# Encoder step: three places for x in the front, the memory's norms spread out, a gate's weights asked for one chunk earlier

## The chip, the cores and the metric

The kernel runs on one core of one Trainium2 chip. The engines named here are TensorE (PE in the rows; PEld is its weight load), VectorE (DVE), ScalarE (ACT), GpSimd (POOL) and SyncE (SP), which only issues DMAs here. The metric is the device time of one launch in microseconds, the median of the runs of a kernel.

## The reference, cut to what matters

The layer takes 1024 prompt tokens and 8 x 16 = 128 sample tokens, width 1024, in fp32. What the change touches is the normed input, its projections, the memory's keys and values, the forget gates and the output gates.

```python
xn = rmsnorm(xp, g_mix[l])
z = xn @ w_in                       # split into qa, ka, va, qb, kb, vb, fl, qm, gates
logf = jax.nn.log_sigmoid(fl.astype(jnp.float32) + b_f.astype(jnp.float32))
...
mk, mv = jnp.split(rmsnorm(mem, g_mem) @ w_mkv, 2, axis=-1)
return rmsnorm(mk.reshape(b, n, H_M, DH_M), g_km), mv.reshape(b, n, H_M, DH_M)
...
o_a = band_attn_prompt(qa, ka, va, rel_bias[l])
o_b = forget_attn_prompt(qb, kb, vb, lf)
o_m = mem_attn(qm, mk, mv)
xp = xp + gated_merge(o_a, o_b, o_m, gates, w_pa[l], w_pb[l], w_pm[l], w_o[l])
xp = xp + sq_relu_mlp(xp, g_ffn[l], w_up[l], w_down[l])
```

The sample tokens go the same way with cached keys and values.

## The kernel before

**Precision.** Most projections are made of three products of fp32r halves: an operand is split into `hi` (rounded) and `lo` (the rest), and TensorE adds hi·whi, hi·wlo and lo·whi in PSUM. ACT makes a `hi`, scaled by the gain where there is one (`gcol`), and DVE the `lo`; `hilo_scaled` does both for one k of 128 rows.

**The front.** x comes in transposed, in five pieces of 256 tokens (`x_load(t)`; piece 4 holds the 128 sample tokens, "the sample tile", token tile 8). Each lands in a place of the arena `FE` (`x_place`) and is split by `x_split(t)` into `xp`. A place is free again when the sums of the piece for the products (`sums`) are made on DVE. The rows of x are loaded a second time, not transposed, by `x_rows`: ACT squares them, POOL takes the root, and `rs` scales what leaves PSUM. Meanwhile TensorE multiplies the token tiles in the order 0, 1, 8, 2 to 7 with the weights of v_a and the forget gates (`wa` and `sb` in the rows; their raw form lies in the arena `RW`); `v_a` evacuates each tile's banks (`z`) on ACT to `zn`, which waits for `rs`, and DVE takes the forget columns to `lf`. All these loads are issued by SP in the order in which the code asks for them, so one that waits for its place holds back all behind it.

**Products and memory.** Four projections follow as `products(...)`, which form sums of weights and of tokens to save matmuls, and then the memory's keys (`mem_products(104, ...)`, with `mem_k`) and values (`mem_products(112, ...)`, with `mem_v`). The work behind a result (`norm`: square on ACT, sum `hss` on DVE, root `hr` on POOL, product `zn` on DVE, transposes `to_T` on TensorE) is put off by `in_(n, ...)` until `flush()` has been called n times, so that TensorE has matmuls between. The places of four raw weights, `kept`, hold their weights longer than others for the products' sums, and x again later: `odd_x(t)` splits the first half of token tile 2t+1 once more from there, during the memory's keys.

**The planned phase.** From the first gate on, each engine's order comes of a planner in the kernel that runs generators against estimated costs (`plan.use`, `plan.op`) and times (`plan.t`). TensorE's filler there are the gates: 24 blocks f of output columns by three chunks c of 384 tokens, 24 matmuls each. `get(f)` asks for the weights of gate f in two halves: ACT issues the DMA into the one staging buffer `wst`, ACT makes `whi` of it and DVE or POOL `wlo`; buffers stand for two gates. Beside them run the band attention ("attention a"), the forget attention, the sample attentions, then the merge with memory attention, and last the output projection and the MLP (L1863), which the change leaves alone. `forget_gates` turns `lf` into log sigmoids, about twenty short operations on DVE, and transposes the result.

PE and DVE follow the order of the code in the front, too, from `in_order.extend((pe, vec))` on. ACT and POOL are ordered by a scheduler there.

## Time and profile before

| | us |
|---|---|
| median of 3 runs | 2014.13 |
| lowest and highest run | 2010.42, 2015.04 |
| profiled execution, whole | 2010.68 |
| its span in the trace | 2008.9 |
| around the span (difference) | 1.78 |
| PE busy in the span | 1954.7 |
| DVE / ACT / POOL busy | 1221.4 / 946.0 / 521.1 |

The profiled execution is near the lowest of the runs. Mean granted TensorE clock over it: 0.989. A row's time is its start from the beginning of the span; "idle before" is the idle time of that engine just ahead of the row, and behind the arrow stands what ended it. The granted clock (PEclk) is a share of full speed, 2.4 GHz.

### The profile page before, as it was taken

How to read it: one execution, taken by the hardware profiler on the slowest of the kernel's cores; microseconds unless marked ns; L12 is line 12 of the kernel's file. 1: busy time of each engine (PE TensorE's matmuls, PEld its weight loads, DVE VectorE, ACT ScalarE, POOL GpSimd, SP SyncE). 2: the span in 40 equal slices, each digit the busy share in tenths (PEclk: the TensorE clock that was granted, in tenths of full speed). 3: DMA queues.
4: the chain of work that ended last, by engine and by line, in shares of the span. 5: the costliest groups of instructions: out<-in, count | busy, mean ns of one | idle time of the engine just before them, and what ended most of it. 6: DMA issues, size and time to landing. Idle time of an engine off the chain costs nothing.

```text
span 2008.9 us, 33955 instructions
## 1 busy us (share of the span) xinstructions
PE 1954.7 (97%) x12338; PEld 1712.1 (85%) x12338; DVE 1221.4 (61%) x2313; ACT 946.0 (47%) x1831; POOL 521.1 (26%) x590
## 2 busy tenths in 40 slices
PE   8999999899999999998899999999999999999999
PEld 8887888788887988887898987889999998888887
DVE  7766657665632555522575843876666665785775
ACT  6645556455643556533452313644444454453332
POOL 3343433332311244311122200244443431000000
PEclk9999999999999999999898999999999999999999
DMA  8555455643259433278658453144343459563463
GB/s 264 162 156 180 117 168 150 203 152 102 80 164 316 154 104 98 68 245 278 196 179 282 153 162 113 46 157 157 127 141 129 143 169 330 183 197 106 128 197 126
DMA packets 223909, 330.54 MB, mean 165 GB/s; under 512 B 32357, under 2 KB 109302, under 8 KB 223742
## 3 DMA queue, kind: packets, MB, share of 16 engines
q1 hardware_dynamic: 166600, 270.44, 42.3%
q10 hardware_dynamic: 57142, 57.93, 8.7%
q8 instruction: 97, 1.59, 0.3%
q14 instruction: 70, 0.57, 0.1%
HBM read 243.11 MB, written 85.18 MB: 163 GB/s over the span
## 4 chain that ended last, share of the span: by engine, by line
PE 77%; DMA 10%; DVE 6%; ACT 2%; issue 2%; POOL 2%; SPq 1%; ACTq 0%; POOLq 0%; DVEq 0%
PE b L1863 36%; PE z L215 28%; PE tp L222 5%; PE tp L215 4%; PE s L215 4%; DMA wst<-in_w_g 2%; DMA th<-tg 1%; POOL fa L203 1%; DVE r L203 1%; DVE fa L203 1%; DVE lo L203 1%; DMA kd<-in_cak 1%; DMA fa<-in_w_up 1%; SPq L203 1%; DMA tg<-tg 1%
## 5 line engine op out<-in xcount | busy, mean ns | idle before, releaser
L1863 PE MATMUL b<-r 128*128 128x512 f32 (+2 forms) x2200 | 457.6, 357 | 4.2 <-ACT r L203 2.1
L1863 PEld LDWEIGHTS b<-r 128*128 128x128 f32 x2200 | 379.6, 190 | 62.6 <-DVE r L203 3.6
L203 ACT ACTIVATE r<-fa 128x512 fp32r<-128x512 f32 (+4 forms) x264 | 212.8, 816 | 327.2 <-PE b L1863 280.9
L203 DVE TENSOR_TENSOR r<-fa,r 128x512 fp32r<-128x512 f32 (+4 forms) x264 | 273.5, 1047 | 136.1 <-ACT r L203 131.9
L215 PE MATMUL z<-hi,whi 128*128 128x384 f32 x960 | 320.2, 365 | 15.0 <-ACT hi L203 8.0
L1863 PE MATMUL b<-r,r 128*128 128x320 f32 (+1 forms) x1928 | 288.3, 299 | 5.8 <-DVE r L203 5.7
L1863 PEld LDWEIGHTS b<-r,r 128*128 128x128 f32 x1928 | 271.2, 190 | 7.7 <-DVE r L203 7.7
L215 PE MATMUL z<-hi,wlo 128*128 128x384 f32 x768 | 262.0, 341 | 0.2
L203 POOL TENSOR_TENSOR fa<-fa 128x512 f32<-128x512 f32 x114 | 165.2, 1455 | 238.4 <-ACT fa L203 125.5
L215 PEld LDWEIGHTS z<-hi,whi 128*128 128x128 f32 x960 | 180.5, 193 | 39.4 <-issue 15.1
L215 PE MATMUL z<-wa,hi 128*128 128x512 f32 (+1 forms) x732 | 203.5, 365 | 6.4 <-ACT hi L203 4.7
L215 PE MATMUL z<-lo,whi 128*128 128x384 f32 x576 | 195.1, 339 | 0.0
L215 PEld LDWEIGHTS z<-wa,hi 128*128 128x128 f32 x732 | 128.7, 192 | 27.2 <-ACT hi L203 5.1
L215 PEld LDWEIGHTS z<-hi,wlo 128*128 128x128 f32 x768 | 146.7, 191 | 1.3 <-DVE wlo L203 1.3
L203 ACT ACTIVATE s<-s,nm 128x256 f32<-128x256 f32 (+8 forms) x180 | 121.2, 679 | 39.1 <-DVE nm L203 38.9
L203 POOL TENSOR_SCALAR s<-s,ri 128x256 f32<-128x256 f32 (+8 forms) x108 | 76.0, 709 | 232.1 <-DVE ri L203 208.7
L215 PE MATMUL z<-wa,lo 128*128 128x512 f32 (+1 forms) x366 | 130.5, 359 | 0.0
L203 DVE CUSTOM_DVE_ANT_0 s<-s,bias 128x384 f32<-128x384 f32 (+4 forms) x144 | 70.4, 526 | 84.3 <-PE s L215 81.3
L215 PEld LDWEIGHTS z<-lo,whi 128*128 128x128 f32 x576 | 109.8, 191 | 0.0
L222 PE MATMUL tp<-ident,s 128*128 128x128 f32 (+1 forms) x680 | 107.3, 277 | 1.7 <-ACT pt L203 1.2
L203 ACT ACTIVATE pt<-tp 128x256 f32<-128x256 f32 (+3 forms) x153 | 66.4, 454 | 80.6 <-PE tp L222 76.8
L203 DVE TENSOR_TENSOR fa<-b,fa 128x256 f32<-128x256 f32 (+1 forms) x160 | 70.5, 448 | 54.0 <-PE b L1863 39.1
(223 smaller groups left out, 3136.4 us busy)
## 6 DMA issues: line engine op xcount, KB each, us to landing
td<-fa SPq DMA_DIRECT2D x112, 256.0 KB
rw<-in_w_in SPq DMA_DIRECT2D x104, 256.0 KB
fa<-td SPq DMA_DIRECT2D x80, 256.0 KB
fa<-in_w_down SPq DMA_DIRECT2D x76, 256.0 KB
fa<-in_w_up SPq DMA_DIRECT2D x32, 512.0 KB
tg<-tg ACTq DMA_DIRECT2D x72, 192.0 KB
th<-tg SPq DMA_DIRECT2D x72, 192.0 KB
wst<-in_w_g ACTq DMA_DIRECT2D x48, 256.0 KB
```

The lines of the kernel that those rows point to most:

```text
L203: ins = f(*a, **k)
L215: ins = nc.tensor.matmul(out, lhsT, rhs, **k)
L222: ins = nc.tensor.transpose(*a)
L1863: pin(nc.tensor.matmul(ps, lh, rh, **k))
```

## The change

It has four parts.

1. **Front.** x has three places in `FE` in place of two (`t % 3`). The rows of x go to `RW` at first, where the raw weights have been used up, and to free parts of `FE` later (`row[1]`). The sample tile is loaded and split ahead of the first rows; piece 2 is asked for after token tile 0, piece 3 after token tile 1, behind the loads of the `kept` weights and two rows.
2. **Memory.** `norm` of a memory tile squares into one of two `zt` buffers in place of the one `sq`; the delays become 3, and the memory's values flush after every k. `odd_x` runs at k = 2 to 5 and uses `hilo_scaled`.
3. **Forget gates.** They begin 30 us later in the planner's time, and their cost is put at 6.0 in place of 3.0.
4. **Gates.** The weights of gate f+1 are asked for at chunk 0 of gate f; before it was chunk 1, but for gate 22's. Gate 23's are asked for at (22, 0) in both.

```diff
--- before.py
+++ after.py
@@ -375,7 +375,7 @@
     def x_place(t):
 
         return FE[:, 4096:5120].rearrange("p (k t) -> p k t", k=8) if t == 4 else \
-            FE[:, t % 2 * 2048:t % 2 * 2048 + 2048].rearrange("p (k t) -> p k t", k=8)
+            FE[:, t % 3 * 2048:t % 3 * 2048 + 2048].rearrange("p (k t) -> p k t", k=8)
 
     def x_load(t, ks=slice(0, 8)):
         sp.dma_start(x_place(t)[:, ks, :], xT[:, ks, t * 256:min(t * 256 + 256, NT)])
@@ -391,7 +391,7 @@
             x += n
 
     def row_sums(src, s, r, e):
-        xt = FE[:, 4096 + e * D:4096 + e * D + D]
+        xt = row[1][:, e * D:e * D + D]
         sp.dma_start(xt, src)
         act.activation(xt, xt, AF.Square, accum_out=s)
         rstd(s, r, D)
@@ -401,7 +401,7 @@
             row_sums(i["x"][t * P:(t + 1) * P, :], ss[:, t:t + 1], rs[:, t:t + 1], row[0])
             row[0] = 1 - row[0]
 
-    row = [1]
+    row = [1, RW]
 
 
 
@@ -590,11 +590,11 @@
             if len(ks) > 1:
                 flush()
 
-    def norm(z, sc, dh, then, gain=None, fresh=False):
+    def norm(z, sc, dh, then, gain=None, fresh=False, lag=2):
 
         nh = HB // dh
         v3 = lambda t: t.rearrange("p (h d) -> p h d", h=nh)
-        sq = tl(pj, (P, HB), tag="sq", bufs=1)
+        sq = tl(pj, (P, 4, P), tag="zt").rearrange("p k t -> p (k t)") if fresh else tl(pj, (P, HB), tag="sq", bufs=1)
         act.activation(sq, z, AF.Square, scale=sc)
         r = tl(pj, (P, 8), tag="hr", bufs=4)
 
@@ -603,7 +603,7 @@
             vec.tensor_reduce(q[:, :nh], v3(sq), AX.X, ALU.add)
             rstd(q[:, :nh], r[:, :nh], dh)
             gps.tensor_scalar(r[:, :nh], r[:, :nh], sc, 1.0, ALU.mult, ALU.mult)
-            in_(2, scale)
+            in_(lag, scale)
 
         def scale():
             zn = tl(pj, (P, HB), tag="zn") if fresh else z
@@ -644,8 +644,8 @@
     def mem_k(t, z):
         def then(zn):
             sp.dma_start(o["mk"][t * P:(t + 1) * P, :], zn)
-            in_(2, lambda: to_T(zn, mkT, t))
-        norm(z, rm[:, t:t + 1], 128, then, g_of["km"], True)
+            in_(3, lambda: to_T(zn, mkT, t))
+        norm(z, rm[:, t:t + 1], 128, then, g_of["km"], True, 3)
 
     mem_v = v_out(o["mv"], rm, True)
 
@@ -721,12 +721,12 @@
         x_load(0, slice(k, k + 1))
         produce((slots + more)[k], vec if k < 2 else gps)
         x_split(0, (k,))
-    x_rows(0)
-    sp.dma_start(bf, i["b_f"].to_broadcast((P, 8)))
     x_load(4)
     x_split(4)
+    x_rows(0)
     x_load(1, slice(0, 4))
     x_load(1, slice(4, 8))
+    sp.dma_start(bf, i["b_f"].to_broadcast((P, 8)))
     x_rows(1)
     x_split(1)
     x_rows(TT - 1)
@@ -735,8 +735,6 @@
         makers_of(pair, PAIRS[n + 1] if n < 2 else None)
     queue.extend(i["w_mkv"][k * P:(k + 1) * P, x:x + HB] for x in (0, HB) for k in range(KD))
     makers.extend([take] * 16)
-    for k in range(4):
-        sp.dma_start(kept[k], rows_(Q_A)(k))
     sp.dma_start(ident, i["ident"])
     for x, y, n in ((0, 128, 128), (128, 384, 128)):
         sp.dma_start(gains[:, x:x + n], i["gains"][0:1, y:y + n].to_broadcast((P, n)))
@@ -762,21 +760,30 @@
             z.append(ps)
         v_a(t, z[0], z[1][:, 0:252])
         vec.scalar_tensor_tensor(lf[:, t, :], z[1][:, 252:260], rs[:, t:t + 1], bf, ALU.mult, ALU.add)
+        if t == 0:
+            x_load(2, slice(0, 4))
+            x_load(2, slice(4, 8))
+            x_rows(2, 3)
+            x_split(2)
         if t in (1, 3, 5):
             for step in sums(t // 2):
                 step()
-            if t < 5:
-                x_load(t // 2 + 2, slice(0, 4))
-                x_load(t // 2 + 2, slice(4, 8))
-                x_split(t // 2 + 2)
-                x_rows(t + 1, t + 2)
             if t == 1:
+                for k in range(4):
+                    sp.dma_start(kept[k], rows_(Q_A)(k))
+                row[1] = RW[:, 6 * UW:]
+                x_rows(4, 5)
+                x_load(3, slice(0, 4))
+                x_load(3, slice(4, 8))
                 ask()
+                x_split(3)
             if t == 3:
+                row[1] = FE[:, 2048:4096]
                 x_rows(6, 7)
+    row[1] = FE[:, 4096:6144]
     for t in range(2):
         row_sums(i["mem"][t * P:(t + 1) * P, :], ss[:, TT + t:TT + t + 1], rm[:, t:t + 1], t)
-    T2, u2, u3 = ([FE[:, (4 * j + t) * HB:(4 * j + t + 1) * HB] for t in range(4)] for j in range(3))
+    u2, u3, T2 = ([FE[:, (4 * j + t) * HB:(4 * j + t + 1) * HB] for t in range(4)] for j in range(3))
     sp.dma_start(tri, i["tri"])
 
     def rs_T():
@@ -801,8 +808,9 @@
     def odd_x(t):
 
         x = kept[t].rearrange("p (k t) -> p k t", k=4)
-        vec.tensor_tensor(x, x, gcol[:, 0, 0:4, None].to_broadcast((P, 4, P)), ALU.mult)
-        into_odd(t, x)
+        h, l = odd(t)
+        for k in range(4):
+            hilo_scaled(x[:, k, :], h[:, k, :], l[k], gcol[:, 0, k:k + 1])
 
     def at_last(t):
 
@@ -831,10 +839,12 @@
                 pe.matmul(ps[t], h, wl, start=False, stop=False)
                 pe.matmul(ps[t], l, wh, start=False, stop=k == KD - 1)
             release(u0 + k)
-            if k % 2:
+            if u0 != 104:
                 flush()
-                if u0 == 104:
-                    odd_x(k // 2)
+            elif k % 2:
+                flush()
+            if u0 == 104 and 1 < k < 6:
+                odd_x(k - 2)
         for t in range(2):
             out(t, ps[t])
 
@@ -848,6 +858,7 @@
 
     def forget_gates(pool):
 
+        yield plan.t + 30.0
         z = lf.rearrange("p t h -> p (t h)")
         n = TT * 8
         w = {k: tl(pool, (P, n), tag="f" + k) for k in "aesuvr"}
@@ -874,7 +885,7 @@
         vec.tensor_tensor(v, v, s, ALU.mult)
         vec.tensor_scalar(z, z, 0.0, None, ALU.min)
         vec.tensor_tensor(z, z, v, ALU.subtract)
-        yield plan.use("vec", 3.0)
+        yield plan.use("vec", 6.0)
         act.dma_start(o["lf"].rearrange("(t p) h -> p t h", p=P), lf)
         bk = plan.take("tp")
         t = tl(psum["tp"], (P, 4, P), tag="tp")
@@ -962,7 +973,7 @@
                 if k == 0:
                     b = plan.take("z")
                     ps = tl(psum["z"], (P, 512), tag="z")
-                    if (f, c) == (22, 0) or c == 1 and f < 22:
+                    if c == 0 and f < 23:
                         plan.spawn(get(f + 1), own=False)
                     if (f, c) == (23, 0):
                         late["start"]()
```

SP's queue in the front, from the last of v_a's weights on (`fe<-in_xT` are pieces of x, `in_x` rows of x, and the `rw<-in_w_in` of 128x512 the kept weights). Before:

```order
L203 DMA fe_268<-in_x 128x1024
L203 DMA bf_210<-in_b_f 128x8
L203 DMA fe_268<-in_xT 128x8x128
L203 DMA fe_268<-in_xT 128x4x256 x2
L203 DMA fe_268<-in_x 128x1024 x2
L203 DMA rw_252<-in_w_in 128x512 x4
...
L203 DMA gq_244<-in_gains 128x1
L203 DMA fe_268<-in_x 128x1024 x2
L203 DMA fe_268<-in_xT 128x4x256 x2
L203 DMA rw_252<-in_w_in 128x512 x6
```

And now:

```order
L203 DMA fe_268<-in_xT 128x8x128
L203 DMA rw_252<-in_x 128x1024
L203 DMA fe_268<-in_xT 128x4x256 x2
L203 DMA bf_210<-in_b_f 128x8
L203 DMA rw_252<-in_x 128x1024 x2
...
L203 DMA gq_244<-in_gains 128x1
L203 DMA fe_268<-in_xT 128x4x256 x2
L203 DMA rw_252<-in_x 128x1024 x3
L203 DMA rw_252<-in_w_in 128x512
L203 DMA rw_252<-in_x 128x1024
L203 DMA rw_252<-in_w_in 128x512 x3
L203 DMA fe_268<-in_xT 128x4x256 x2
```

The sample tile's load stands ahead of the first row, piece 2 directly behind the constants, and the kept weights behind piece 2; piece 3 comes behind them.

ACT in the front, from the last split of v_a's weights (`sb`) on (`hi_163` and `hi_164` are the sample tile, `hi_143`, `hi_144`, `hi_153` and `hi_154` piece 1, `ss` the sums of squares). Before:

```order
L203 ACTIVATE sb_264<-rw_252 128x520
L203 ACTIVATE fe_268,ss_243<-fe_268 128x1024
L203 ACTIVATE sa_260<-fe_268 128x512
L203 ACTIVATE zn_476<-z_426,rs_241 128x260
L203 ACTIVATE zn_476<-z_451,rs_241 128x252
L203 ACTIVATE hi_163_231<-fe_268,gcol_201 128x128 x4
L203 ACTIVATE hi_164_232<-fe_268,gcol_201 128x128 x4
L203 ACTIVATE hi_143_211<-fe_268,gcol_201 128x128 x4
```

And now:

```order
L203 ACTIVATE sb_264<-rw_252 128x520
L203 ACTIVATE hi_163_231<-fe_268,gcol_201 128x128 x4
L203 ACTIVATE hi_164_232<-fe_268,gcol_201 128x128 x4
L203 ACTIVATE rw_252,ss_243<-rw_252 128x1024
L203 ACTIVATE hi_143_211<-fe_268,gcol_201 128x128 x4
...
L203 ACTIVATE rw_252,ss_243<-rw_252 128x1024
L203 ACTIVATE hi_154_222<-fe_268,gcol_201 128x128 x4
L203 ACTIVATE rw_252,ss_243<-rw_252 128x1024
L203 ACTIVATE zn_472<-z_422,rs_241 128x260
L203 ACTIVATE zn_472<-z_447,rs_241 128x252
```

The eight `hi` of the sample tile moved ahead of the first square; the evacuation of token tile 0 (`zn`) moved behind 24 `hi` and three squares.

TensorE at the end of the memory's values and the begin of gate 0 (`wa,sa` are the values' matmuls, one row of three for each of two tiles and each k; `tp<-ident,zn` transposes the memory's normed keys). Before:

```order
L215 MATMUL z_3696<-wa_256,sa_260 128x512 x3
L215 MATMUL z_3697<-wa_256,sa_260 128x512 x3
L215 MATMUL z_3696<-wa_256,sa_260 128x512 x3
L215 MATMUL z_3697<-wa_256,sa_260 128x512 x3
L222 MATMUL tp_3785<-ident_203,zn_3747 128x128 x4
L222 MATMUL tp_3793<-ident_203,zn_3751 128x128 x4
L215 MATMUL z_3839<-hi_143_211,whi_3775 128x384
```

And now:

```order
L215 MATMUL z_3704<-wa_256,sa_260 128x512 x3
L215 MATMUL z_3705<-wa_256,sa_260 128x512 x3
L222 MATMUL tp_3769<-ident_203,zn_3743 128x128 x4
L222 MATMUL tp_3777<-ident_203,zn_3747 128x128 x4
L215 MATMUL z_3704<-wa_256,sa_260 128x512 x3
L215 MATMUL z_3705<-wa_256,sa_260 128x512 x3
L215 MATMUL z_3839<-hi_143_211,whi_3799 128x384
```

The transposes moved ahead of the last k. The forget gates' transpose moved the other way: some 256 matmuls later, from the second chunk of gate 0 into attention a.

## Rows read from the trace of the kernel before

**Rows 1.** The page, part 1: busy time, share of the span and instructions of each engine.

```profile
PE 1954.7 (97%) x12338; PEld 1712.1 (85%) x12338; DVE 1221.4 (61%) x2313; ACT 946.0 (47%) x1831; POOL 521.1 (26%) x590
```

**Rows 2.** Timeline of PE in the front: start us, us, instruction, idle before.

```profile
22.43 0.75 PE L215 MATMUL z<-wa,hi 128*128 128x260 f32 x4 [2.55 <-ACT hi L203]
...
43.77 1.10 PE L215 MATMUL z<-wa,hi 128*128 128x260 f32 x5 [2.13 <-ACT hi L203]
```

**Rows 3.** Windows, PE alone: length, PE busy (matmuls started), PEclk, DMA share, GB/s.

```profile
23.70:27.20 3.50, 3.50 (x19) 0.51 0.39 128
27.20:30.70 3.50, 3.50 (x31) 1.00 0.99 323
44.20:47.70 3.50, 3.50 (x19) 0.51 1.06 398
```

**Rows 4.** Timeline of ACT in the front.

```profile
21.98 6.24 ACT L203 ACTIVATE hi<-fe,gcol 128x128 fp32r<-128x128 f32 x21
...
43.21 1.70 ACT L203 ACTIVATE hi<-fe,gcol 128x256 fp32r<-128x256 f32 x4 [0.23 <-DMA fe<-in_xT]
```

**Rows 5.** Timeline of DVE in the front.

```profile
21.40 0.69 DVE L203 TENSOR_TENSOR sa<-fe,sa 128x512 fp32r<-128x512 f32 x1
...
22.73 2.18 DVE L203 SCALAR_TENSOR_TENSOR lo<-fe,gcol,hi 128x128 fp32r<-128x128 f32 x8
```

**Rows 6.** The chain that ended last, in the front: start us, us, what.

```profile
36.14 7.05 DMA fe<-in_xT
```

**Rows 7.** Timeline of PE where the memory ends and the gates begin.

```profile
375.87 3.05 PE L215 MATMUL z<-wa,sa 128*128 128x512 f32 x12 [0.59 <-DVE wa L203]
380.11 2.81 PE L215 MATMUL z<-wa,sa 128*128 128x512 f32 x11 [1.19 <-DVE wa L203]
384.61 0.63 PE L222 MATMUL tp<-ident,zn 128*128 128x128 f32 x4 [1.68 <-DVE zn L203]
386.36 1.08 PE L222 MATMUL tp<-ident,zn 128*128 128x128 f32 x4 [1.12 <-DVE zn L203]
399.62 0.31 PE L222 MATMUL tp<-ident,lf 128*72 128x128 f32 x1 [1.78 <-DVE lf L203]
407.61 0.45 PE L215 MATMUL z<-hi,whi 128*128 128x384 f32 x1 [0.90 <-ACT whi L203]
```

**Rows 8.** Windows there: PE, PEld, DVE, ACT, POOL busy (x), PEclk, DMA share, GB/s.

```profile
385.50:392.50 7.00, 6.11 (x20) 5.40 (x21) 2.33 (x5) 2.96 (x6) 0.00 (x0) 0.51 0.75 253
...
400.00:411.00 11.00, 9.99 (x56) 9.35 (x55) 4.80 (x9) 3.93 (x8) 0.29 (x2) 1.00 0.62 175
```

**Rows 9.** Timeline of ACT there.

```profile
381.35 0.69 ACT L203 ACTIVATE sq<-z,rm 128x512 f32<-128x512 f32 x1 [2.82 <-DVE hss L203]
...
387.48 0.35 ACTq L203 DMA_DIRECT2D wst<-in_w_g  x1
...
390.64 0.63 ACT L203 ACTIVATE whi<-wst 128x512 fp32r<-128x512 f32 x1 [0.86 <-DMA wst<-in_w_g]
```

**Rows 10.** Timeline of DVE in the forget gates: the first operation, and one of eight `TENSOR_SCALAR fv`.

```profile
391.91 0.19 DVE L203 TENSOR_SCALAR fa<-lf 128x72 f32<-128x72 f32 x1
...
397.10 1.32 DVE L203 TENSOR_SCALAR fv<-fv 128x72 f32<-128x72 f32 x1
```

**Rows 11.** Windows of attention a and behind it, columns as in rows 8.

```profile
411.00:450.00 39.00, 37.53 (x268) 32.33 (x266) 26.10 (x88) 24.50 (x63) 15.13 (x19) 1.00 0.45 146
...
450.00:600.00 150.00, 149.26 (x1135) 127.93 (x1135) 75.44 (x266) 83.62 (x213) 37.00 (x57) 1.00 0.34 110
```

**Rows 12.** Timeline of PE in the last gates.

```profile
925.02 0.69 PE L215 MATMUL z<-hi,whi 128*128 128x384 f32 x1 [2.99 <-ACT whi L203]
```

**Rows 13.** Timeline of ACT in the last gates.

```profile
909.25 0.34 ACTq L203 DMA_DIRECT2D wst<-in_w_g  x1
```

**Rows 14.** Window behind the wait of rows 12, columns as in rows 8.

```profile
925.00:928.50 3.50, 3.48 (x22) 2.21 (x22) 0.85 (x2) 0.68 (x2) 0.70 (x1) 0.53 0.90 289
```

**Rows 15.** Timeline of POOL beside the forget gates.

```profile
397.01 1.28 POOL L203 TENSOR_TENSOR kl<-ld,kh 128x512 fp32r<-128x512 f32 x1 [12.25 <-DMA wst<-in_w_g]
```

## The prediction, made before the changed kernel ran

> **What bounds the kernel now.** I read the page first: TensorE is busy 1954.7 us, 97% of the span, and no other engine comes over 61% [rows 1]. So the end moves only by what TensorE waits, and by the clock at which it works. Next I read TensorE's timeline for rows with an idle time before them, up to the end of the gates. In the front there are two of weight, 2.55 us before the sample tile (token tile 8) and 2.13 us before token tile 4, both released by a `hi` of ACT [rows 2]. Six more, 7.26 us in sum, lie between 375 and 408 us, where the memory's projection ends and the gates begin [rows 7].
>
> Then the windows around them, for the clock. Behind the 2.55 us stall TensorE ran 3.5 us at 0.51 of full speed, the lower of its two levels (1.2 of 2.4 GHz), and started 19 matmuls where 31 start in the 3.5 us after; behind the 2.13 us stall it is 19 again [rows 3]. The 12 missing matmuls at 3.5/31 = 0.113 us are 1.35 us, so such a stall costs its idle time and about 1.35 us more. Behind the two stalls before the memory's transposes the clock was at 0.51 for 7 us, with TensorE busy 6.11 [rows 8]. At 0.49 x 6.11 that would be 3.0 us; in the front the same sum gives 1.7 where the counts say 1.35, so I take 0.8 of it, 2.4 us. The gate region further on has almost nothing left to win: from 450 to 600 us TensorE is idle 0.74 us [rows 11].
>
> **The change, part by part.**
>
> *The sample tile.* Before, ACT does a row's square, a split of raw weights and two evacuations before the tile's first `hi` at 21.98 [rows 4], and DVE makes a sum of weights and one of x (two rows between 21.40 and 22.73) before the first `lo` [rows 5]. After, ACT's eight `hi` stand right behind the last v_a weight split, and DVE's `lo` right behind the row that ends at 21.40 here. TensorE came free at 22.43 - 2.55 = 19.88. ACT is no longer the one waited for, since the tile's load goes out ahead of the row now; DVE's first `lo` is ready at 21.40 + 0.27 = 21.7 and TensorE wants it two matmuls (0.23 us) after 19.88. What is left is about 1.5 us, or 1.4 if the earlier load pays a little; the bounds are 0 and the old 2.55. Whether a slow stretch follows a wait of 1.4 us these two do not tell; behind the 1.78 us at 399.62 [rows 7] the next 11 us ran at full clock [rows 8]. So I count the slow stretch as gone: gain 2.55 - 1.4 + 1.35 = 2.5 us.
>
> *Token tile 4.* Before, the load of x tile 2 has to wait for the sums that free its place; it is issued at 36.14, takes 7.05 us [rows 6], and ACT's `hi` starts at 43.21 [rows 4]. With a third place it only waits until the sample tile is split (DVE's eight `lo` from 22.73 last 2.18 us [rows 5]) and until SP has come past three row loads and the small constants. The third of those rows reuses the place of the first and waits for its square, which is a 1 us operation standing behind the eight `hi`. I put the issue at 27 to 29 us and the landing at 34 to 36. TensorE wants the tile at 41.64 less the 2.5 us just gained, 39.1. It costs nothing as long as the issue is before 39.1 - 7.05 = 32. Both the idle time and the slow stretch go: 2.13 + 1.35 = 3.5 us. The cover has a price: evacuating tile 0 stands behind 24 `hi` and three squares on ACT now, and its bank is free within a few tenths of when TensorE asks for it (8 `hi` of 0.30 us are 2.4 us by [rows 4], so one misplaced group costs that). Bounds for this: 0 and 2.4; I take 0 because DVE's `lo` paces the same stretch at 0.27 each. Front: **6.0 us**, bounds 2.2 (those 2.4 lost, with a slow stretch of 1.35) and 7.4 (nothing left of either stall).
>
> *The end of the memory.* Before, the square of the second memory tile starts only at 381.35, after DVE has reduced the first (one buffer) [rows 9]; the reduction, POOL's root and two products follow, and TensorE waits 1.68 and 1.12 us for `zn` behind the last product [rows 7]. After, the squares have a buffer each, a step of the delayed work is done behind every k instead of every second one, and the transposes stand ahead of the last k. The 0.59 and 1.19 us for `wa` come of ACT's queue, which is held by the gate's DMA issue; it stands later now. The 1.78 us for the forget gates' transpose leave this place, and the 0.90 us for `whi` go, because gate 1 is asked for at (0,0). One wait stays: a single staging buffer. The second half of gate 0's weights is asked for once the first is split, and from issue at 387.48 to `whi` at 390.64 it takes 3.16 us [rows 9]. The four k of the first half are 12 matmuls of 384 columns, 0.113 us [rows 3] x 384/260 = 0.17 each and 2.0 us together, and they cover that much of it if the second request goes out as they begin. With the late start of `wlo` I keep 1.4 us, between 0 and 3.2. So 7.26 - 1.4 + 2.4 = 8.3 us, less 0.3 for `odd_x` (four short ACT operations per tile where one long one stood, and one DVE multiply fewer, in mem_k, where TensorE is fed): **8.0 us**, bounds 4 (3.2 us of waiting kept, and the slow stretch) and 9.7.
>
> The Trainium skill ("SBUF — State Buffer", The DMA setup-cost knee) puts a transfer at about 2 us and its bytes over 436 GB/s, an estimate of 2.6 us for these 256 KB. The row shows 3.16 with the whi's own start in it, so the trace is slower than that, and by the page's price the wait kept would be about 0.8 us instead of 1.4 and the sum 0.6 us better.
>
> *The forget gates.* Their chain of some twenty short DVE operations ran from 391.91 to the transpose at 399.62, where TensorE waited for it [rows 7, 10]. Put 30 us later it stands inside attention a, where DVE is busy 26.1 of 39 us and TensorE idles only 1.47 [rows 11]. Its DVE work, 20 operations of about 0.22 us or 4.4 us, must fit into 12.9 us of gaps. Nothing in the trace has this chain beside attention. The lower bound is 0, if the gate matmuls between cover it; the upper is its whole 7.7 us. TensorE's rows there are mostly gate matmuls that wait for nobody, so I am nearer to the low end: **-1.5 us**.
>
> *Gates asked for a chunk earlier.* For gates 1 to 21 this is hidden now (0.74 us idle in 150), so nothing is won. At the end, gate 23's second half makes TensorE wait 2.99 us [rows 12], with a slow stretch behind it [rows 14]. Its first half is issued at 909.25 [rows 13], at (22,0), which the change leaves as it is; but gate 22 is out of the staging buffer earlier. Between 0 and 2.99 + 1.35 = 4.3 us I take **1.0**.
>
> Sum: 6.0 + 8.0 + 1.0 - 1.5 = 13.5 us. Against the profiled execution (2010.68) that is 1997.2. The median of the runs shown is 3.45 us above that execution, which is near the lowest run; I add half, 1.7, and forecast **1998.9**.
>
> **The rivals.**
>
> *Gates that block ACT (slower).* A request one chunk earlier means that `whi` waits in ACT's queue for TensorE to finish gate f-1, whose buffers it writes, and for the DMA behind the single staging buffer. If ACT stands still while attention's exponentials queue behind it, TensorE waits in each of 22 gates. It decides from 13.5/22 = 0.6 us per gate on; at the 0.90 us that TensorE once waited for a `whi` [rows 7] it would be 20 us, so 1998.9 + 20 = 2019. Against it: buffers for two gates, and the last reader of gate f-1 ends right where gate f begins, so the wait for TensorE is nearly nil. Chance 0.06.
>
> *The forget chain is not covered.* Beside POOL's work the DVE operations stretch: one of them, of the kind that takes 0.19 us at 391.91, took 1.32 at 397.10 while POOL ran a 1.28 us product [rows 10, 15]. POOL is busy 15.13 of 39 us in attention a [rows 11], so of 20 operations some eight would meet one, at half its mean of 15.13/19 = 0.8 us: 3 us more on a chain of 7.7. If attention waits for all that, 5 to 6 us are lost instead of 1.5 and the time is 2003. Chance 0.15. The Trainium skill ("SBUF — State Buffer", SBUF: two separate sides) calls the port pair of DVE and GpSimd an exclusive lock on which the later one blocks fully; by that rule, the 1.32 us row agrees.
>
> *The front's wait returns elsewhere.* x tile 3 is now issued behind four kept weights and two rows; or ACT's evacuation of tile 0 is late. Then one stall of about 2.4 us with its 1.35 comes back: 2003. Chance 0.13.
>
> *It does little.* The memory's end is bound by staging through one buffer, not by the norms: then about 4 of its 8 us come, and 2003 again; with the two rivals above on top of it, 2011, no change. Chance 0.10 for the first alone.
>
> **How the numbers follow.** The forecast as it stands has 0.50, the three cases at 2003 0.38 together, two or three of them at once (2007 to 2013) 0.06, the slower rival 0.06. A measurement of this kernel can tell about 0.2%, 4 us, from no change. Faster by that means under 2010.1: 0.50 + 0.38, less 0.03 of the cases at 2003 that lose more besides, and 0.02 of the combined ones, 0.87; within it 0.07; slower 0.06. The best end takes every term at its bound, 7.4 + 9.7 + 4.3 = 21.4, or 1991.0 with the 1.7; the worst that I keep inside is two rivals together, 2007. With a microsecond on either side, since the runs of before lie 4.6 us apart, the range is 1990 to 2008; 0.05 stay below it and 0.12 above.
>
> **What would show it.** In the profile after: an idle time of under 2 us at the sample tile, none before tile 4, and the granted clock full from 20 to 60 us, with the front's last matmuls some 6 us earlier. No `zn` wait between the memory and the gates, one wait of 1 to 2 us for gate 0's second `whi`, and full clock there. Attention a should end not more than 2 us later relative to its start. I am wrong if TensorE idles 0.5 us or more per gate between 450 and 900 us, if a new stall with a slow stretch stands in the front or in attention a, or if the end moves by less than 6 us.

## The result, and the profile after

The changed kernel takes 1993.59 us (median of 4 runs, 1989.31 to 1995.43) against 2012.67 us before (4 runs). The ratio is 0.990, with a 95% interval of 0.988 to 0.992: 19.1 us faster. The profiled execution is the fastest of the four, 1989.31 us, its span 1987.5, and its mean granted clock 0.996 where before had 0.989. In the experiments below one of the ten runs of the memory alone, 2759.39 us at a granted clock of 0.64, is left out of its ratio.

The page of the changed kernel, part 1:

```profile
PE 1943.9 (98%) x12338; PEld 1704.7 (86%) x12338; DVE 1225.3 (62%) x2305; ACT 947.9 (48%) x1844; POOL 535.9 (27%) x593
```

TensorE's timeline of the changed kernel where [rows 2] and [rows 7] had their waits, and the last v_a matmul of the front (`z<-sb,lo`):

```profile
22.16 0.39 PE L215 MATMUL z<-wa,lo 128*128 128x260 f32 x1 [1.38 <-DVE lo L203]
...
61.76 0.28 PE L215 MATMUL z<-sb,lo 128*128 128x260 f32 x1
...
374.43 0.66 PE L222 MATMUL tp<-ident,zn 128*128 128x128 f32 x4 [0.69 <-ACT zt L203]
374.85 1.62 PE L215 MATMUL z<-wa,sa 128*128 128x512 f32 x6
376.31 0.34 PE L215 MATMUL z<-hi,whi 128*128 128x384 f32 x1
...
399.25 0.33 PE L222 MATMUL tp<-ident,s 128*128 128x128 f32 x1 [1.04 <-POOL s L203]
...
425.58 0.28 PE L222 MATMUL tp<-ident,lf 128*72 128x128 f32 x1 [1.05 <-DVE lf L203]
...
472.31 0.44 PE L222 MATMUL tp<-ident,s 128*128 128x128 f32 x2 [1.43 <-ACT pt L203]
```

The wait at the sample tile is 1.38 us and ends with a `lo` of DVE, the one before token tile 4 is gone. The six waits of [rows 7] are gone from their places; ahead of the first gate one new wait of 0.69 us, for ACT's `zt`, is left. The transpose of `lf` waits 1.05 us in its new place, where it waited 1.78 in the old one.

The same stretches as in [rows 3] and [rows 8] in the changed kernel (PE alone in the first two lines: length, PE busy with matmuls started, PEclk, DMA share, GB/s; all engines in the third):

```profile
23.70:27.20 3.50, 3.50 (x32) 1.00 0.44 126
44.20:47.70 3.50, 3.50 (x32) 1.00 0.93 306
```

```profile
385.50:392.50 7.00, 7.00 (x42) 7.00 (x42) 3.09 (x5) 2.73 (x5) 1.32 (x7) 1.00 0.75 230
```

32 matmuls started where there were 19, and TensorE was fed throughout the stretch behind the memory.

To see where the 21.4 us between the two profiled spans lie, I cut each span at three rows that every kernel here has, with the same TensorE work between them (the same number of matmuls in each stretch): the start of the last `z<-sb,lo` (end of v_a in the front), of the first `z<-hi,whi` (gate 0) and of the first `b<-whi,hi` (output projection). For the changed kernel these are 61.76 and 376.31 above and this row of its timeline:

```profile
1152.51 0.39 PE L1874 MATMUL b<-whi,hi 128*128 128x512 f32 x1
```

| profile | front | to gate 0 | gates, attentions, merge | output projection, MLP |
|---|---|---|---|---|
| before | 68.23 | 318.86 | 785.31 | 836.5 |
| changed | 61.76 | 314.55 | 776.20 | 835.0 |
| difference | -6.5 | -4.3 | -9.1 | -1.5 |

The last column is code that the change does not touch. In all fourteen profiles of this study it lies between 834.2 and 842.3 us, so that a span alone cannot tell a few microseconds. The third column tells somewhat more. Kernels of this study with the same order on TensorE behind gate 0 differ there by up to 3.8 us: 785.31, 784.16, 781.49 and 782.94 for before, the front, the memory and both; 776.20 and 779.76 for the changed kernel and the one with the old `odd_x`, which differ by two instructions there. A single difference under some 4 us is therefore not shown. Columns of the table are differences of such row starts, the last one up to the span's end.

### The profile page after: what moved, and what is told of

The parts are those of the page before. It is cut to its first block, busy times and chain, and to the rows that moved or that the text cites. A ratio compares the mean times of both kernels' runs of the same rounds, so it can differ in the third digit from the quotient of the medians.

```text
span 1987.5 us, 33936 instructions
## 1 busy us (share of the span) xinstructions
PE 1943.9 (98%) x12338; PEld 1704.7 (86%) x12338; DVE 1225.3 (62%) x2305; ACT 947.9 (48%) x1844; POOL 535.9 (27%) x593
## 5 line engine op out<-in xcount | busy, mean ns | idle before, releaser
L215 PE MATMUL z<-hi,whi 128*128 128x384 f32 x960 | 315.1, 360 | 6.5 <-DVE th L203 2.2
L203 POOL TENSOR_SCALAR s<-s,ri 128x128 f32<-128x128 f32 (+8 forms) x101 | 68.9, 687 | 228.2 <-DVE ri L203 208.9
```

The source lines that it names most:

```text
L203: ins = f(*a, **k)
L215: ins = nc.tensor.matmul(out, lhsT, rhs, **k)
```

## The experiments

Times are from runs taken beside the kernel before, in three rounds, each on one chip; ratios go with their 95% intervals. The changed kernel was not run again beside them, so a comparison with its 0.990 is one across chips. Profiles are of one execution.

**Each part alone.** The parts as they stand in the list of the change: the front; the memory; the forget gates' two lines; the gates' one condition. For the last two the edits to before are

```diff
+        yield plan.t + 30.0
-        yield plan.use("vec", 3.0)
+        yield plan.use("vec", 6.0)
```

and

```diff
-                    if (f, c) == (22, 0) or c == 1 and f < 22:
+                    if c == 0 and f < 23:
```

> Of the change only the front: three places for x, the new order of loads, rows and splits. The order of every engine from the memory on is that of before. Theory (each part gains at its own place, and the gains add up): TensorE is 7.2 us earlier at 130 us, as in the changed kernel's trace, nothing more is won or lost later, and the time falls by 7 us from that of before. Rival (the large gains at gate 23 and at the start of the merge, some 10 us together in the changed kernel, come of everything being earlier, not of the order): the merge gains too, and the time falls by 12 us or more.

> Of the change only the memory: the squares in two buffers, the longer delays, the flush at every k, odd_x by hilo_scaled. Theory: the waits for zn (2.80 us) and for wa (1.78 us) go, and with them the slow stretch of some 2.4 us; two short waits for zt near 350 us cost 1.3 us; the waits for lf and for gate 1's whi stay. The time falls by 5 to 6 us. Rival (the transposes' place does not decide, a single staging buffer holds gate 0): one wait takes the place of the others and the time falls by less than 2 us.

> Of the change only the forget gates: 30 us later in the plan and a higher planned cost, which changes the order of TensorE's rows from the first gate to the last. Theory: the wait of 1.78 us for lf goes and attention a loses about as much, so that the time is within 2 us of before; what differs at gate 23 and in the merge is not of this part. Rival A (chain not covered): 4 us slower. Rival B (the new order is what helps the merge): 6 us or more faster, with the waits between 955 and 970 us gone.

> Of the change only the earlier request of a gate's weights. Theory: the wait of 0.90 us for gate 1 goes and of the 2.99 us and the slow stretch at gate 23 two to four us go; with the merge unchanged the time falls by 3 to 5 us. Rival A (ACT blocked by whi): TensorE idles at each gate and the time rises by 4 us or more. Rival B (this is what frees the merge, whose first weights come through the same engines): 8 us or more faster, no slow stretch between 960 and 980 us.

| kernel | ratio | front | to gate 0 | gates to merge | rest |
|---|---|---|---|---|---|
| front alone | 0.9962 (0.9947 to 0.9976) | 61.43 | 316.09 | 784.16 | 836.7 |
| memory alone | 0.9976 (0.9962 to 0.9990) | 68.67 | 314.86 | 781.49 | 835.8 |
| forget gates alone | 0.9965 (0.9945 to 0.9984) | 68.26 | 318.13 | 774.33 | 834.5 |
| gates alone | 0.9985 (0.9970 to 0.9999) | 68.19 | 318.45 | 782.16 | 834.2 |

The front gave 7.6 us (0.38% of 2008.65) and the memory 4.8, near the 7 and the 5 to 6 of the theory. The forget gates' two lines gave 7.0 us (3.2 to 11.0), where the theory had the time within 2 us of before and rival B said 6 or more: it is rival B. All of it, 11.0 us in the profile, lies between gate 0 and the output projection. (In this one profile the granted clock reads 0.95 instead of 1.00 nearly throughout, and yet its untouched last column, 834.5 us, is among the shortest; so this reading did not go with a longer time.) The earlier request of the gates' weights gave 3.0 us (0.2 to 6.0); in its profile the merge's large waits for `hi` are gone, but a wait of 2.88 us at 635 us, with 6.8 us at half clock, and one of 3.24 us for `of` at 929 us came in. So its own expectation holds in size and not in place, and its 3.2 us in the third column are within the spread of one order.

**Is it the order or the earlier time?** Neither the front nor the memory moves an instruction on TensorE behind gate 0; both other parts do, up to the merge. So front and memory together keep the old order and start it 10 us earlier (gate 0 at 377.48 instead of 387.09). Two more kernels take the forget part's lines one by one. (The 0.1 and 1.3 us of other work in two of the expectations are counted from TensorE's order behind the last gate, at the spacing of such rows in before.)

> Front and memory together, so that the order of the planned phase stays that of before. Theory (these two gains add, and the rest of the gain is the new order): first gate some 11 us earlier than before, 375.5 to 377 us; from the first gate to the first matmul of the output projection 780 to 784 us, against 785.3 before and 776.2 in the changed kernel; the time 11 to 13 us under before. Rival (what comes later is gained by being earlier): that stretch is 777 or less and the time 17 us under.

> Before, with only the line that starts the forget gates 30 us later in the plan; their cost stays 3.0. Its order at the start of the merge is that of the forget part alone. Theory (what counts is where the order puts the last gates, sample attention and the first merge blocks): the stretch from the first gate to the output projection is 774 to 778 us, as with the whole forget part (774.3). Rival (the higher planned cost does it, by leaving room on DVE): 782 or more.

> Before, with only the planned cost of the forget gates at 6.0; they start where they did before, so that nothing is moved out of TensorE's way at 400 us. But the numbers shift the plan, and at the start of the merge TensorE has 1.3 us of other work ahead of the first merge blocks, as in the changed kernel, where before has 0.1. Theory (any shift of the plan that changes this place takes the merge's stalls away; the delay is not needed): the stretch from the first gate to the output projection is 775 to 781 us. Rival (the delay itself wins it): 784 to 787 us, no change.

| kernel | ratio | front | to gate 0 | gates to merge | rest |
|---|---|---|---|---|---|
| front and memory | 0.9952 (0.9933 to 0.9971) | 61.45 | 316.03 | 782.94 | 842.3 |
| delay alone | 0.9984 (0.9964 to 1.0003) | 68.92 | 317.44 | 773.64 | 840.1 |
| cost alone | 0.9965 (0.9948 to 0.9981) | 68.72 | 316.93 | 779.33 | 835.5 |

With the old order the third column stays at 782.9, so being earlier is not it. The delay line alone gives the whole 11.7 us there. Its time, 0.9984, shows much less, and its interval reaches from 7.2 us faster to 0.6 slower: the profile has 840.1 us in the untouched last column and a wait of 3.38 us at token tile 4 with 6.8 us of half clock, and the profiled execution took 2001.87 us where the median of its runs is 2007.00. So that one is clear by stage in one execution and not shown by time. The planned cost alone, with the chain left where it was, gives 6.0 us against before, which is 2.2 under the lowest of the old order, and 7.0 us by time (3.8 to 10.5). So a shift of the plan that moves nothing out of TensorE's way gives a part of it, too; how large a part, the spread does not tell.

**Where in that stretch.** TensorE's timeline of front and memory together (old order) in the last gates and the merge:

```profile
913.26 0.69 PE L215 MATMUL z<-hi,whi 128*128 128x384 f32 x1 [2.99 <-ACT whi L203]
...
957.13 0.69 PE L215 MATMUL z<-hi,whi 128*128 128x384 f32 x1 [2.95 <-ACT hi L203]
...
1042.53 0.69 PE L215 MATMUL z<-hi,whi 128*128 128x384 f32 x1 [2.30 <-ACT hi L203]
```

and its windows behind these three (PE alone):

```profile
912.60:919.40 6.80, 6.14 (x29) 0.50 0.88 302
957.00:963.80 6.80, 6.36 (x18) 0.50 0.57 179
1042.30:1052.50 10.20, 8.98 (x34) 0.50 1.04 407
```

The same three places in the kernel that has the new order of the forget part, and the old request of weights (the next experiment):

> The changed kernel without its last part: a gate's weights are asked for at chunk 1 again, as before. Front, memory and forget gates as in the changed kernel. Theory (the gain behind the gates' begin is the new order, and the forget part's alone suffices): first gate at 376 to 378 us; the stretch from the first gate to the output projection 773 to 778 us, against 776.2 in the changed kernel and 782.9 with front and memory alone; the time within 4 us of the changed kernel's. Rival (the earlier request is needed, since without it gate 23 and the merge stall): 781 us or more, 6 us slower.

> The changed kernel without the forget part: the chain stands at the gates' begin again. Theory (the request at chunk 0 alone gave 782.2 us for the stretch, of which 2.7 us were the wait for lf at 400 us and one wait of 2.9 us with a slow stretch stood at 635 us): 779 to 783 us, 3 to 6 us slower than the changed kernel. Rival (any new order will do): 776 to 778 us, no difference.

```profile
910.35 0.44 PE L215 MATMUL z<-hi,whi 128*128 128x384 f32 x1 [1.28 <-ACT whi L203]
...
947.76 0.44 PE L215 MATMUL z<-hi,whi 128*128 128x384 f32 x1 [0.79 <-ACT hi L203]
948.83 0.44 PE L215 MATMUL z<-hi,whi 128*128 128x384 f32 x1 [0.64 <-POOL hi L203]
...
1032.47 0.45 PE L215 MATMUL z<-hi,whi 128*128 128x384 f32 x1 [0.79 <-DVE hi L203]
```

```profile
905.00:915.00 10.00, 8.61 (x95) 1.00 0.86 297
949.90:953.30 3.40, 3.32 (x11) 0.50 0.77 280
1032.00:1043.00 11.00, 10.14 (x66) 1.00 1.03 390
```

Waits of 2.99, 2.95 and 2.30 us became 1.28, 1.43 in two pieces and 0.79. But right behind the last window the new order has a wait that the old one has not, for DVE's `th`, and a slow stretch behind it:

```profile
1044.63 0.62 PE L215 MATMUL z<-hi,whi 128*128 128x384 f32 x2 [2.02 <-DVE th L203]
```

```profile
1045.50:1048.90 3.40, 3.40 (x15) 0.50 0.94 307
```

So 23.8 us of half clock became 6.8 there, and 2.7 us of waiting went. To see how much of the 8.7 us between 782.94 and 774.20 lies here, the third stretch is cut once more, at the first matmul of gate 22, which has the same matmuls ahead of it in both but for one. The rows, old order first, and the windows of the whole stretch:

```profile
899.51 0.44 PE L215 MATMUL z<-hi,whi 128*128 128x384 f32 x1
...
896.99 0.42 PE L215 MATMUL z<-hi,whi 128*128 128x384 f32 x1
```

```profile
377.48:1160.42 782.94, 759.97 (x5715) 0.98 0.53 172
...
376.14:1150.34 774.20, 756.32 (x5714) 0.99 0.53 173
```

1.1 us lie ahead of gate 22 (899.51 - 377.48 less 896.99 - 376.14) and 7.6 in the last two gates and the merge. Over the whole stretch TensorE waits 5.1 us less (22.97 against 17.88), and its matmuls take 3.7 us less; that the clock makes these 3.7 is argued: 23.8 us of it ran at half clock, against 6.8 and 3.4 more near 393 us.

| kernel | ratio | front | to gate 0 | gates to merge | rest |
|---|---|---|---|---|---|
| changed, without the gates part | 0.9928 (0.9900 to 0.9957) | 61.61 | 314.53 | 774.20 | 837.0 |
| changed, without the forget part | 0.9945 (0.9929 to 0.9960) | 61.81 | 315.72 | 782.77 | 839.5 |

Both columns came out as the theory said. The times can be set against the changed kernel's only by ratios from two chips, 0.9928 and 0.9945 against 0.9902: some 5 and 9 us slower, where the theory had up to 4 and 3 to 6. Without the forget part the third column is 782.77, the same as with front and memory alone: the earlier request of weights gives nothing there by itself, and on top of the forget part it does not help either (776.20 with, 774.20 without). Sorted by the order on TensorE behind gate 0, the third column is 781.5 to 785.3 us in the four kernels with the old order, 782.2 and 782.8 in the two with the gates part alone, 774.2 and 774.3 in the two with the forget part alone, and 776.2 and 779.8 in the two with both. By time the forget part on front and memory is 0.9952 less 0.9928, 4.8 us, and the two intervals overlap. The profiled execution of front and memory took 2004.45 us with a median of 2001.51, that of the kernel without the gates part 1989.14 with a median of 1996.11, so the 8.7 us are rather too many than too few.

**What the merge's waits are.** In before, with five staging places for the merge:

```diff
-            yield from staged((wpool[0], late["mf"]), src, wt, at, ("w", x), ring=("st", 3))
+            yield from staged((wpool[0], late["mf"]), src, wt, at, ("w", x), ring=("st", 5))
...
-                    pool, ring, tag = (late["os"], ("ost", 6), "wst") if "os" in late else (late["mf"], ("st", 3), "wst")
+                    pool, ring, tag = (late["os"], ("ost", 6), "wst") if "os" in late else (late["mf"], ("st", 5), "wst")
```

> Before, with five staging places in place of three for the merge's weights and operands. TensorE's order at the merge's start still puts only 0.1 us of other work ahead of the first two blocks. Theory (the stalls of 2.04 and 3.56 us between 960 and 970 us and the slow stretch behind them are a matter of weights that are asked for too late): they fall under 2 us in sum, and the stretch from the first gate to the output projection is 780 us or less. Rival (not the places but the transfers, which share the DMA engines with the sample attention's caches): the stalls stay above 4 us.

The two waits in before, on TensorE, and what ACT's operations ahead of them waited for (`oTa` is the output of attention a, loaded back as an operand; `in_w_pa` a weight):

```profile
964.52 0.44 PE L215 MATMUL z<-hi,whi 128*128 128x384 f32 x1 [2.04 <-ACT hi L203]
...
969.29 0.69 PE L215 MATMUL z<-hi,whi 128*128 128x384 f32 x1 [3.56 <-ACT hi L203]
```

```profile
963.94 0.52 ACT L203 ACTIVATE hi<-wst 128x384 fp32r<-128x384 f32 x1 [2.73 <-DMA wst<-oTa]
...
967.67 0.63 ACT L203 ACTIVATE whi<-wst 128x512 fp32r<-128x512 f32 x1 [3.21 <-DMA wst<-in_w_pa]
```

With five places the ratio is 0.9948 (0.9929 to 0.9967), the third column 776.28. At the begin of the merge this is all that TensorE waits for over half a microsecond:

```profile
968.01 0.44 PE L215 MATMUL z<-hi,whi 128*128 128x384 f32 x1 [0.81 <-DVE hi L203]
```

So the waits were for what comes through three places too late: first an operand, then an operand that stands on ACT behind a weight. The gate's wait of 2.95 us stays in this kernel at 927.77. The same edit on the changed kernel:

> The changed kernel with five staging places in place of three for the merge's weights and operands. Theory (the places gave before 9 us between the first gate and the output projection, by the merge's stalls; the changed kernel has only 1 to 3 us of such waits left there): the stretch is 773 to 776 us, and the time 0 to 3 us under the changed kernel's. Rival (places and order each give their full gain): 768 us or less, 8 us faster.

The ratio is 0.9942 (0.9925 to 0.9959); front 63.98, to gate 0 317.83, gates to merge 783.62, rest 836.7. Theory and rival both fail: the third column is 7.4 us longer. (The front and the stretch to gate 0, which this edit leaves alone, are 5.5 us longer in this profile, too.) TensorE now waits 2.02 us for gate 23's `whi`, 1.84 for `ptl`, 1.55 for `th` and 2.23 for `spt`. More places help one order and, in this profile, hurt the other. No version here beats the changed kernel's 0.990.

**The memory's part.** The changed kernel with `odd_x` as before:

```diff
-        h, l = odd(t)
-        for k in range(4):
-            hilo_scaled(x[:, k, :], h[:, k, :], l[k], gcol[:, 0, k:k + 1])
+        vec.tensor_tensor(x, x, gcol[:, 0, 0:4, None].to_broadcast((P, 4, P)), ALU.mult)
+        into_odd(t, x)
```

> The changed kernel with odd_x as before (one multiply on DVE, one long operation on ACT, four subtractions on DVE), still at k = 2 to 5. TensorE's order is the same. Theory (the sixteen short ACT operations hold up zt, for which TensorE waits 0.61 and 0.31 us near 350 us and loses 1.3 us in all there): those waits go and the first gate comes 0.8 to 1.5 us earlier, at 375 us. Rival (the waits come of the squares that take zt's two buffers): no change, within 0.3 us of 376.3.

Both are wrong. Gate 0 comes at 383.63, 7.3 us later, and the ratio is 0.9972 (0.9954 to 0.9989); the third column is 779.76, the rest 837.9. Not all of the 7.3 us is of `odd_x`: the same transposes, ahead of `odd_x`'s first operation, already start 4.5 us later (the first row is of the changed kernel):

```profile
320.22 0.60 PE L222 MATMUL tp<-ident,fe 128*128 128x128 f32 x4
...
324.75 0.60 PE L222 MATMUL tp<-ident,fe 128*128 128x128 f32 x4
```

That leaves 2.8 us from there to gate 0. The waits for `zt` near 350 us did go, as the theory had it, but larger ones came. DVE's timeline of this kernel around the memory's keys shows why:

```profile
369.97 0.90 DVE L203 TENSOR_TENSOR lo<-rw,hi 128x128 fp32r<-128x128 f32 x4 [1.31 <-ACT hi L203]
...
371.39 0.69 DVE L203 TENSOR_TENSOR rw<-rw,gcol 128x512 f32<-128x512 f32 x1
373.38 0.90 DVE L203 TENSOR_TENSOR lo<-rw,hi 128x128 fp32r<-128x128 f32 x4 [1.30 <-ACT hi L203]
374.19 1.89 DVE L203 TENSOR_TENSOR wa<-rw,wa 128x512 fp32r<-128x512 f32 x3
376.00 1.27 DVE L203 TENSOR_REDUCE hss<-zt 128x4 f32<-128x512 f32 x2
```

In the old form DVE multiplies, ACT copies, DVE subtracts, and DVE stands in its queue until ACT has answered: 0.70, 0.70, 1.31 and 1.30 us in four tiles. The reduction of the norms comes at 376.00, and TensorE waits 1.74 us for `wa` and 0.89 and 1.12 for `zn` again. In the changed kernel DVE's `lo` waits for nothing and the reductions are at these rows of its timeline:

```profile
364.55 1.13 DVE L203 SCALAR_TENSOR_TENSOR lo<-rw,gcol,hi 128x128 fp32r<-128x128 f32 x4
...
367.41 0.68 DVE L203 TENSOR_REDUCE hss<-zt 128x4 f32<-128x512 f32 x1
368.91 0.69 DVE L203 TENSOR_REDUCE hss<-zt 128x4 f32<-128x512 f32 x1 [0.82 <-ACT zt L203]
```

The front is 1.9 us longer in this profile, and this looks like rival three of the prediction seen once. x tile 3 was issued at 39.90 instead of 38.66, and TensorE waited 0.91 us for a `hi` of ACT at 51.46. Ahead of that `hi` ACT had stood 4.24 us in an evacuation that waited for the store of an earlier one, so the late evacuation is the nearer cause:

```profile
50.18 0.84 ACT L203 ACTIVATE zn<-z,rs 128x260 f32<-128x260 f32 x2 [4.24 <-DMA out_va<-zn]
50.91 0.51 ACT L203 ACTIVATE hi<-fe,gcol 128x256 fp32r<-128x256 f32 x1
```

Behind the front TensorE waited 1.55 us more, for a `wa` of ACT at 65.45. Why this edit, which acts some 300 us later, changes that, the runs do not show.

## Why the prediction was right, and which of its terms were not

*The sample tile.* Right in mechanism and size: 1.38 us left against 1.4, released by `lo`, and the clock at 1.00.

*Token tile 4.* Right. The load was issued at 26.20 (forecast 27 to 29), the wait and the slow stretch went, and the evacuation of tile 0 started at 28.34, with no wait of TensorE for its bank. The front's 6.0 us measured 6.5.

*The end of the memory.* 8.0 us were forecast, and this term is too large. Alone, it brings the output projection forward by 1172.40 - 1165.02 = 7.4 us (4.8 by time); on top of the front, only by 1161.68 - 1160.42 = 1.3 in the profiles. The two parts overlap, and the sum counts the waits for `wa` fully for the memory: with the front alone the waits for `wa` were gone already and gate 0 came 2.8 us sooner than the front explains. The wait that I kept for gate 0's second half was 0: asked for at 374.16, its `whi` began on ACT at 377.58 and took 0.62 us, and TensorE did not wait for it. And the step on `odd_x` was wrong in sign: I took 0.3 us off for more operations on ACT, where the new form, at its new places k = 2 to 5, gives some 3 us by ending DVE's waits for ACT. (With the front alone the old form at its old places cost no more: gate 0 at 377.52, against 377.48 with the memory's part added.) Front and memory together: 14.0 forecast, 12.0 measured up to the output projection in the profiles, 9.7 by the ratio of the runs.

*The forget gates.* This is the step that failed, "-1.5 us". At its own place the loss was small, and smaller than I had it: the chain took from 412.20 to 425.43, 13.2 us where it was 7.7, and TensorE waited 1.05 us for it, where [rows 7] have 1.78. Two more waits, of 1.04 and 1.43 us, stand in attention a of the changed kernel, but nothing ties them to the chain: the kernel without the gates part has the chain in the same place and no wait of over half a microsecond between 394 and 670 us. What I priced was the operations where they were moved to, and not the order behind them. The plan's shift took waits out of gate 23 and two places of the merge, 500 us later, and the part is worth 11.0 us alone (785.31 less 774.33), 8.7 on front and memory (782.94 less 774.20) and 6.6 on all other parts (782.77 less 776.20). By time it is 7.0 us alone and 4.8 on front and memory.

*The gates.* "1.0" was for gate 23. Alone the part gives 3.0 us by time, but on front and memory it gives 0.2 in the third column, and on front, memory and forget gates it costs 2.0. On top of the other parts it is worth nothing that these runs can tell. The slower rival fell: TensorE idles 5.4 us between 411 and 600 us in the changed kernel, where before had 2.2, at the waits for `lf` and `pt` above and at two for a DMA (1.56 and 1.39 us), none for `whi`. Between 450 and 900 us it idles 8.3 us over 18.5 gates, under the 0.5 us per gate that the prediction had named as a sign of being wrong. Another of these signs did appear: the wait of 1.43 us for `pt` lies in attention a, whose last output is stored at 564.79, and a slow stretch of 3.4 us stands behind it.

*The sum.* 13.5 against 21.4 between the profiles: front 6.5, up to gate 0 4.3, the third stretch 9.1, 1.5 of untouched code. In the third stretch my terms had only the waits for `lf` and `whi`, a part of the slow stretch, the 1.4 us kept, the -1.5 and the 1.0, about 1 to 3 us together; the merge was in none of them. By the runs it is 19.1 us against a forecast of 15.2 from 2014.13. That the time, 1993.6, lies inside the range is in part luck: the memory's term was too large by 2 to 4 us, the gain of the new order was missing, and the two partly cancel. The lower end of the range was made of every term at its best, not of that gain.

*DVE beside POOL.* The rival of the uncovered chain gave its mechanism rightly. DVE's and POOL's timelines of the changed kernel in attention a:

```profile
418.26 0.73 DVE L203 TENSOR_TENSOR fu<-fs 128x72 f32<-128x72 f32 x1
419.03 1.18 DVE L203 TENSOR_SCALAR fv<-fu 128x72 f32<-128x72 f32 x1
420.24 0.23 DVE L203 TENSOR_TENSOR fv<-fv,fu 128x72 f32<-128x72 f32 x1
```

```profile
418.11 0.80 POOL L203 TENSOR_SCALAR s<-s,ri 128x640 f32<-128x640 f32 x1
418.88 1.27 POOL L203 TENSOR_TENSOR ql<-ld,qh 128x512 fp32r<-128x512 f32 x1
```

An operation that takes 0.20 us elsewhere in this chain takes 1.18 while POOL runs its 1.27, and the next one 0.23 when POOL is done. The Trainium skill ("SBUF — State Buffer", SBUF: two separate sides) says that a GpSimd operation and a DVE operation, the latter in a 2-port mode or (against a GpSimd operation that reads SBUF) with two inputs in SBUF, hold a shared port pair one after the other, the later one blocked until the first is through; the trace agrees, with DVE's 1.18 us ending at 420.21 and POOL's 1.27 at 420.15. Whether this operation runs in such a mode, the trace does not tell. Part of the chain's 13.2 us is something else: from 412.8 to 416.3 us DVE did attention's operations. The stretch cost TensorE little, since it had other matmuls.

**What stays open.** The runs show that the order behind gate 0 makes some 5 to 11 us (6.6 to 11.0 by the third column, 4.8 to 7.0 by time), and that staging places take the merge's waits away in the old order. They do not show by what step the new order does it, nor why five places make the new order worse. Whether a different delay would win more was not tried.

## What to carry to other kernels

Where a planner sets the order, a change of one cost or start time has to be priced over all that the plan orders after it: compare the orders up to the end, and read every wait behind the place, not only the place. Cut the spans at rows that all kernels share; a part's gain is then seen in its stretch, and noise of untouched code stays in its own. Look first how far the stretch varies among kernels with the same order. In this kernel a split that goes from DVE to ACT and back to DVE in order held DVE for ACT's answer, 0.70 to 1.31 us each time; the one that reads the source on both engines did not.

## What the runs showed of the hardware that was not expected

The length of the last wait does not tell whether the half clock follows. In the changed kernel the 1.43 us before 472.31 were followed by 3.4 us at 0.50, and without the gates part waits of 0.79 and 0.64 us at 948 us by the window shown above, while before ran 11 us at full clock behind 1.78 us [rows 7, 8]. The untouched MLP shows it best. At one place of it TensorE has the same two waits in before, in the changed kernel and with the gates part alone: 1.04 or 1.05 us for ACT's `r`, and 1.8 us later 1.39 to 1.41 for DVE's. In before 6.8 us at half clock come there, in the changed kernel 3.4, and with the gates part alone none. The windows (PE alone) are before's, the changed kernel's and that of the gates part alone, with its two rows:

```profile
1310.60:1317.40 6.80, 6.48 (x23) 0.50 0.10 36
```

```profile
1293.40:1296.80 3.40, 3.40 (x15) 0.50 0.00 0
```

```profile
1306.25 0.42 PE L1863 MATMUL b<-r 128*128 128x320 f32 x1 [1.04 <-ACT r L203]
1308.07 0.42 PE L1863 MATMUL b<-r,r 128*128 128x320 f32 x1 [1.40 <-DVE r L203]
```

```profile
1308.00:1314.80 6.80, 6.55 (x43) 1.00 0.11 37
```
